# Column-tiled products issued in whole groups, state outputs four tiles side by side, and a buffer of its own for the S5 parameter scratch

## The chip, the cores and the metric

The kernel runs on one core of one Trainium2 chip. Its time is that of the device, in microseconds (us), from one execution of the whole program; several executions are timed and their median is compared. Engines are named as in the profile: PE is TensorE (PEld its weight loads), DVE is VectorE, ACT is ScalarE, POOL is GpSimd, SP is SyncE, which here only issues DMA transfers.

## The reference

One layer of a decoder works on 256 prompt tokens and 64 sample tokens (eight sequences of eight) with the same weights, model width 2048, all in float32. Cut to what the change touches:

```python
h = _rmsnorm(x, p['norm_mix'])
z = h @ p['w_in']                       # one projection of 11280 columns, split into:
u_s5, q_g, k_g, v_g, r_g, a_low, q_x, gate_logits = jnp.split(z, ...)
# S5: 64 groups of 16 channels, each with 64 complex states; h_re, h_im from a scan over time
bu_re = jnp.einsum('blgc,gpc->blgp', ug, bbar_re)      # and bu_im
y = (jnp.einsum('blgp,gcp->blgc', h_re, c_re)
     - jnp.einsum('blgp,gcp->blgc', h_im, c_im) + d_skip * ug)
# attention over 256 memory tokens, 4 heads of 256; the sample has its own cached keys and values
scores = jnp.einsum('blhd,bmhd->bhlm', qh, mem_k) * (XA_HEAD_DIM ** -0.5)
o = jnp.einsum('bhlm,bmhd->blhd', jax.nn.softmax(scores, axis=-1), mem_v)
# then gated linear attention, the merge of the three branches, w_out, and a SwiGLU of 5632
```

The memory keys and values of the prompt are themselves a product of the normalised memory with `w_mem_k` and `w_mem_v`, and are outputs too.

## The kernel before

Activations lie with features on the 128 partitions and the 320 tokens as columns. A block of weights of 128 x 2048 (a unit) is loaded by SP into one of three `raw` buffers, and `parts` (L73 to L81) makes two numbers of each: `whi` (a cast on ACT, L79) and `wlo` (the rest, a subtraction on DVE, L80), two buffers of each. `mm3` (L87 to L93) multiplies them with activations that are split in the same way: three matmuls per 128 rows (L91, L92, L93), 48 for a unit of 16 blocks. `proj` is one unit of `w_in` with the activations `hh` and `hl`.

The program has three parts. `front` (L205) makes the memory's values (8 steps, L298 to L300) and keys (8 steps, `kT`, L342), and during the keys writes the normalised input: it scales a block (L348, DVE), casts it to `hh` (ACT) and subtracts to `hl` (DVE, both in `split`, L1066 and L1067). Beside it POOL works out the parameters of the S5 branch (`s5_params`, L365): some 140 small operations, then the doublings of the rotation table (L508 to L511) and the input map `bb` (L498 to L500). These use a scratch tile, `s5_scr`, that before the change has the tag `hl`: it lies in the very buffer in which `hl` is written afterwards (L243, L334). So the first `hl` has to wait until POOL has read `s5_scr` for the last time.

`body` (L1024) advances three generators, each with its share of steps: `main` (the attention over the memory, `attn`, for four heads, then the gated linear attention, `gla`), `s5` (eight tiles of 128 channels, `s5_tile`) and `gates` (48 projections). A scheduler with a model of times then puts the instructions of each engine in order. PE works off its order strictly: an instruction that waits holds all behind it. `back` (L1069) is merge, output projection and feed forward, nothing but units with `mm3`.

Some products are column-tiled: the stationary operand has only 32 columns, the product uses one of four 32-column strips of the array (`tile_position=(0, 32 * c)`), and four products that stand next to each other on four strips can run at the same time. They are in float32, and each one is two MATMUL rows in the trace. There are four kinds:

- `yp` (L654): outputs of the S5 states, 4 tiles of states times real and imaginary part, 8 products of 320 columns for each of 8 tiles of channels. Before, a tile goes through in two halves (`JB = 2`): after each half two tiles of states are multiplied, so no more than two strips are ever in use, in the order part 0 of both, part 1 of both.
- the sample's keys (L749) and values (L770) in `attn`: 16 products of 256 columns each, for each of 4 heads: two sets `g` of four sequences `c`, accumulated over two blocks. Keys and values come by DMA in pieces of two sequences into `at_kv`, three buffers (L739).
- the decay input (L809) and the sample's states in `gla` (L962), which the change leaves as they are.

Each is an instruction of its own to the scheduler, which may put others between them.

Of the kernel before, what the change touches and what calls it, by code (L numbers as in the profile page):

```python
# [49 lines left out]
class Build:  # L50
# [32 lines left out]
    def unit(self, src, n=2048):  # L83
        """A block of weights in two parts that sum to it exactly."""
        return self.parts(self.load(src, n), n)
# [8 lines left out]

    def psum_mm(self):
        # the banks of the small products serve too once those are over
        self.turn += 1
        if self.wide and self.turn % 2:
            return self.psum_sm()
        return self.pmm.tile([P, 512], F32, name="pmm", tag="pmm", bufs=2)  # L100
# [11 lines left out]
    def rstd_tok(self, out, sums, n, scale):  # L112
        """out[token, tile] = 1 / sqrt(scale sum over partitions of sums + eps); sums may be several."""
# [16 lines left out]
        # a step of third order, then one of Newton's  # L130
# [10 lines left out]
    def spread(self, r, n):  # L141
        """PSUM [128, n]: r[token, tile] in the columns of its tokens, on all partitions."""
# [9 lines left out]
    def rstd(self, sums, n, scale):  # L152
        """The same by columns, in PSUM; sums has whole tiles of columns."""
# [4 lines left out]
    def build(self):  # L158
        nc, tc, io = self.nc, self.tc, self.io
        with ExitStack() as es:  # L160
# [18 lines left out]
            # the activation table is loaded before the first operands come  # L179
            early = cp.tile([P, 1], F32, name="early")  # L180
            nc.scalar.activation(early[:], self.ones[:, 0:1], AF.Copy, scale=1.0)
            # the tensor engine's clock rises with use, ahead of the first operands
# [7 lines left out]
            # scan resets of a chunk of the prompt and of the sample  # L190
# [14 lines left out]
    def front(self):  # L205
# [37 lines left out]
        params = self.s5_params(mp, hp.tile([P, KD * NT], F32, name="s5_scr", tag="hl", bufs=1))  # L243
# [8 lines left out]
        def load(i):  # L252
            """Weights of a step; with the first four, the memory of the same rows."""
# [28 lines left out]
        def products(i):  # L282
# [5 lines left out]
            # values: tokens on partitions  # L288
# [22 lines left out]
        with self.tc.manual_schedule(engines={mybir.EngineType.SP}):  # L311
            load(0)
            load(1)
            for i in range(16):
# [15 lines left out]
                if i == 6:  # L330
# [3 lines left out]
                    self.hl = hp.tile([P, KD, NT], F32R, name="hl", tag="hl", bufs=1)  # L334
# [6 lines left out]
                # keys: features on partitions  # L341
# [23 lines left out]
    def s5_params(self, tp, scr):  # L365
        """Decay, rotations and input map of the states, 64 of a group on 64 partitions."""
# [44 lines left out]
        # sine and cosine: reduced by multiples of pi/2, then polynomials  # L411
# [40 lines left out]
        # sin = sg (s ev + c odd), cos = sg (c ev - s odd)  # L452
# [15 lines left out]
        # reciprocal, from its bits and by Newton steps  # L468
# [16 lines left out]
        # rotations, first 16 steps of all states  # L485
        for n in (1, 2, 4, 8):
            self.double(self.tab1, 32, n, *(scr[:, o : o + 64 * n] for o in (2048, 2048 + 512)), V)

        # input and output maps, two groups of channels side by side
# [12 lines left out]
    def double(self, tab, nj, n, x, y, V):  # L502
        """Steps n+1..2n of the rotations in tab from steps 1..n."""
# [9 lines left out]
    def s5_prep(self, ut):  # L513
        """Input of one tile of 128 channels and the map of its four tiles of states."""
# [6 lines left out]
        # products of 32 channels: rows hi, lo, hi of u by rows hi, hi, lo of the map  # L521
# [29 lines left out]
    def s5_tile(self, ut, prep):  # L551
        """Generator over the steps of one tile of 128 channels, four tiles of states."""
# [14 lines left out]
        # |a| e^(i theta CH): carries a state from a chunk to the next  # L567
# [6 lines left out]
        # initial states of the sample, turned to the positions in its chunk  # L574
# [14 lines left out]
        yp = self.pmm.tile([P, 512], F32, name="yp", tag="yp", bufs=1)  # L589
        for r0 in range(0, 4, JB):  # L590
# [42 lines left out]
            hp = []  # L633
            for i in range(JB):
# [7 lines left out]
                h = sp.tile([P, 2, NT], F32, name="s5_h", tag="s5_h", bufs=2)  # L642
# [8 lines left out]
            for part in range(2):  # L651
                for i in range(JB):
                    r = r0 + i
                    nc.tensor.matmul(  # L654
                        yp[32 * r : 32 * r + 32, :NT], self.cT[:, part, r, :], hp[i][:, part, :],
                        start=part == 0, stop=part == 1, tile_position=(0, 32 * r),
                    )
            if r0 + JB < 4:
                yield
        y = self.y1[:, ut, :]  # L660
# [19 lines left out]
    def attn(self, h):  # L680
# [9 lines left out]
        def softmax(ps, n, rows):  # L690
            """Rows of ps[:rows, n, 256] to probabilities in SBUF."""
# [16 lines left out]
        # prompt  # L708
# [27 lines left out]
        # sample: keys as [b, d-tile, mem], values as [b, mem-tile, d]; four sequences side by side,  # L736
        # each in 32 rows of which the first 8 count
        def cache(b, which):
            kv = ap.tile([P, 2, 512], F32, name="at_kv", tag="at_kv", bufs=3)  # L739
# [4 lines left out]
        for g in range(2):  # L744
            kv = [cache(4 * g, 0), cache(4 * g + 2, 0)]
            for i in range(2):
                for c in range(4):
                    b = 4 * g + c
                    nc.tensor.matmul(  # L749
                        ps[32 * c : 32 * c + 32, g * 256 : (g + 1) * 256],  # L750
                        q[:, i, NP_ + b * SL : NP_ + b * SL + 32], kv[c // 2][:, c % 2, i * 256 : (i + 1) * 256],
                        start=i == 0, stop=i == 1, tile_position=(0, 32 * c),
                    )
# [577 lines left out]
```

## Time and profile before

| | us |
|---|---|
| median of three runs | 2143.52 (2142.88 to 2143.59) |
| span of the profiled execution, first to last instruction | 2141.8 |
| PE busy | 2113.7 (99%) |
| DVE busy | 1293.9 (60%) |
| ACT busy | 849.1 (40%) |
| POOL busy | 147.1 (7%) |

For the profiled execution only its span is given; the runs' median is 1.7 us longer, which lies ahead of the first and behind the last instruction. Busy time is the union of an engine's instructions. A matmul's listed duration runs to its modelled end and overlaps with the next one's; what PE spends on one is read from the distance of two starts.

### The profile page before, as it was taken

To read this page: it belongs to the slowest core of one execution; us is meant where nothing else is said; L and a number is where in the kernel's file an instruction comes from. 1 tells how busy PE (TensorE), PEld (TensorE's weight loads), DVE (VectorE), ACT (ScalarE), POOL (GpSimd) and SP (SyncE) were. 2 spreads that over 40 slices of the span, in tenths; PEclk is the share of its full clock that TensorE was granted. 3 is DMA by queue.
4 is the path that set the end of the run, shared out by engine and by line. 5 is a ranking of instruction groups with operands and counts; after the bars stand their busy time and mean duration, and the time that the engine had idled before them with its cause. 6 is when DMAs were issued, how large, how long until landed. Compare 5 with 4: busy or idle time off the path is not lost.

```text
span 2141.8 us, 34011 instructions
## 1 busy us (share of the span) xinstructions
PE 2113.7 (99%) x14404; PEld 2047.6 (96%) x14404; DVE 1293.9 (60%) x1964; ACT 849.1 (40%) x1117; POOL 147.1 (7%) x203
## 2 busy tenths in 40 slices
PE   9899999999999999999999999999999999999997
PEld 7799898989999999999999999999999999999997
DVE  7768769898897864675555444444444444444444
ACT  6444344564444333554433333233322333233343
POOL 8511011011011000000000000000000000000000
PEclk9899999999999999999999999999999999999998
DMA  9565654436345454675554444454435443444442
GB/s 331 198 218 196 212 212 166 155 130 198 128 156 172 134 187 151 219 242 194 188 206 143 150 141 146 136 172 154 141 128 167 158 153 124 149 170 153 145 135 104
DMA packets 72697, 362.23 MB, mean 169 GB/s; under 512 B 8032, under 2 KB 18144, under 8 KB 42720
## 3 DMA queue, kind: packets, MB, share of 16 engines
q1 hardware_dynamic: 72544, 360.05, 49.3%
q8 instruction: 113, 1.85, 0.4%
q14 instruction: 40, 0.33, 0.0%
HBM read 338.49 MB, written 21.53 MB: 168 GB/s over the span
## 4 chain that ended last, share of the span: by engine, by line
PE 94%; POOL 3%; DVE 1%; ACT 1%; issue 1%; DMA 0%; DVEq 0%; POOLq 0%
PE pmm L93 20%; PE pmm L91 20%; PE pmm L92 19%; PE psm L91 10%; PE psm L93 10%; PE psm L92 10%; PE yp L654 1%; PE bu L600 0%; PE psm L770 0%; PE psm L749 0%; PE psm L896 0%; POOL s_ep L384 0%; PE psm L712 0%; PE psm L730 0%; DVE wlo L80 0%
## 5 line engine op out<-in xcount | busy, mean ns | idle before, releaser
L79 ACT CAST whi<-raw 128x2048 fp32r<-128x2048 f32 (+3 forms) x308 | 538.8, 1750 | 945.8 <-issue 542.8
L80 DVE TENSOR_TENSOR wlo<-raw,whi 128x2048 fp32r<-128x2048 f32 (+3 forms) x308 | 649.6, 2110 | 293.1 <-ACT whi L79 287.4
L93 PE MATMUL pmm<-hh,wlo 128*128 128x320 f32 x1408 | 439.8, 312 | 0.0
L91 PE MATMUL pmm<-hh,whi 128*128 128x320 f32 x1408 | 439.5, 312 | 0.0
L92 PE MATMUL pmm<-hl,whi 128*128 128x320 f32 x1408 | 438.1, 311 | 0.0
L93 PEld LDWEIGHTS pmm<-hh,wlo 128*128 128x128 f32 x1408 | 264.5, 188 | 10.1 <-issue 9.2
L91 PEld LDWEIGHTS pmm<-hh,whi 128*128 128x128 f32 x1408 | 264.6, 188 | 7.5 <-issue 6.6
L92 PEld LDWEIGHTS pmm<-hl,whi 128*128 128x128 f32 x1408 | 264.5, 188 | 5.2 <-issue 4.8
L91 PE MATMUL psm<-fh,whi 128*128 128x320 f32 x704 | 217.6, 309 | 0.0
L91 PE MATMUL pmm<-fh,whi 128*128 128x320 f32 x704 | 217.6, 309 | 0.0
L92 PE MATMUL pmm<-fl,whi 128*128 128x320 f32 x704 | 217.6, 309 | 0.0
L93 PE MATMUL psm<-fh,wlo 128*128 128x320 f32 x704 | 217.5, 309 | 0.0
L92 PE MATMUL psm<-fl,whi 128*128 128x320 f32 x704 | 217.5, 309 | 0.0
L93 PE MATMUL pmm<-fh,wlo 128*128 128x320 f32 x704 | 217.5, 309 | 0.0
L91 PEld LDWEIGHTS psm<-fh,whi 128*128 128x128 f32 x704 | 132.1, 188 | 0.1
L92 PEld LDWEIGHTS pmm<-fl,whi 128*128 128x128 f32 x704 | 132.1, 188 | 0.0
L91 PEld LDWEIGHTS pmm<-fh,whi 128*128 128x128 f32 x704 | 132.1, 188 | 0.0
L93 PEld LDWEIGHTS pmm<-fh,wlo 128*128 128x128 f32 x704 | 132.1, 188 | 0.0
L92 PEld LDWEIGHTS psm<-fl,whi 128*128 128x128 f32 x704 | 132.1, 188 | 0.0
L93 PEld LDWEIGHTS psm<-fh,wlo 128*128 128x128 f32 x704 | 132.1, 188 | 0.0
L93 PE MATMUL pmm<-hidh,wlo 128*128 128x320 f32 x352 | 109.2, 310 | 0.0
L91 PE MATMUL psm<-hidh,whi 128*128 128x320 f32 x352 | 108.8, 309 | 0.0
(431 smaller groups left out, 3707.8 us busy)
## 6 DMA issues: line engine op xcount, KB each, us to landing
raw<-w_in SPq DMA_DIRECT2D x88, 1024.0 KB, 5.0
raw<-w_fg SPq DMA_DIRECT2D x44, 1024.0 KB, 4.9
raw<-w_fu SPq DMA_DIRECT2D x44, 1024.0 KB, 4.9
raw<-w_fd SPq DMA_DIRECT2D x64, 704.0 KB, 4.1
raw<-w_br SPq DMA_DIRECT2D x24, 1024.0 KB, 4.9
at_kv<-kv SPq DMA_DIRECT2D x32, 512.0 KB, 4.3
raw<-w_out SPq DMA_DIRECT2D x16, 1024.0 KB, 4.9
raw<-w_mk SPq DMA_DIRECT2D x8, 1024.0 KB, 5.3
```

The lines of the kernel that those rows point to most:

```text
L79: nc.scalar.copy(hi[:, s], raw[:, s])
L80: nc.vector.tensor_tensor(lo[:, s], raw[:, s], hi[:, s].bitcast(F32), op=ALU.subtract)
L91: nc.tensor.matmul(ps, hi[:, ws], xh[:, kx + k, :], start=k == 0, stop=False)
L92: nc.tensor.matmul(ps, hi[:, ws], xl[:, kx + k, :], start=False, stop=False)
L93: nc.tensor.matmul(ps, lo[:, ws], xh[:, kx + k, :], start=False, stop=k == nk - 1)
L654: nc.tensor.matmul(yp[32 * r : 32 * r + 32, :NT], self.cT[:, part, r, :], hp[i][:, part, :], start=part == 0, stop=part == 1, tile_positio ...
```

## The change

Three edits. First, a helper `together` gives its first product to the scheduler and asks that the others be issued right after it. The keys' products of a head are given as one group of 16, and so are the values'; the group starts with the product that needs the piece loaded last (`g = 1`, `c = 3`). All four pieces of keys (or values) are loaded first, and `at_kv` has four buffers instead of three. Second, the outputs of the states are no longer multiplied after each half: the four `s5_h` of a tile are kept (four buffers instead of two), and eight products follow as one group, imaginary part first, four strips side by side. Third, `s5_scr` gets a tile of its own, 2048 wide, in the pool of `front`; the doublings use its columns 1024 to 2047, the same that the input map uses for its two products, so the map's first product now stands behind the doublings on POOL. The scratch that the program keeps for DMA descriptors is set to 1024. Comments and docstrings are gone, which shifts line numbers by 7 or 8.

```diff
+    def together(self, products):
+        first = products[0]().ins
+        with self.tc.issue_after(first):
+            for p in products[1:]:
+                p()
...
-        params = self.s5_params(mp, hp.tile([P, KD * NT], F32, name="s5_scr", tag="hl", bufs=1))
+        params = self.s5_params(mp, mp.tile([P, 2048], F32, name="s5_scr"))
...
-                    self.hl = hp.tile([P, KD, NT], F32R, name="hl", tag="hl", bufs=1)
+                    self.hl = hp.tile([P, KD, NT], F32R, name="hl")
...
         for n in (1, 2, 4, 8):
-            self.double(self.tab1, 32, n, *(scr[:, o : o + 64 * n] for o in (2048, 2048 + 512)), V)
+            self.double(self.tab1, 32, n, *(scr[:, o : o + 64 * n] for o in (1024, 1536)), V)
...
-        yp = self.pmm.tile([P, 512], F32, name="yp", tag="yp", bufs=1)
+        hp = []
         for r0 in range(0, 4, JB):
...
-            hp = []
             for i in range(JB):
...
-                h = sp.tile([P, 2, NT], F32, name="s5_h", tag="s5_h", bufs=2)
+                h = sp.tile([P, 2, NT], F32, name="s5_h", tag="s5_h", bufs=4)
...
-            for part in range(2):
-                for i in range(JB):
-                    r = r0 + i
-                    nc.tensor.matmul(
-                        yp[32 * r : 32 * r + 32, :NT], self.cT[:, part, r, :], hp[i][:, part, :],
-                        start=part == 0, stop=part == 1, tile_position=(0, 32 * r),
-                    )
             if r0 + JB < 4:
                 yield
+        yp = self.pmm.tile([P, 512], F32, name="yp", tag="yp", bufs=1)
+        self.together([
+            lambda part=part, r=r: nc.tensor.matmul(
+                yp[32 * r : 32 * r + 32, :NT], self.cT[:, part, r, :], hp[r][:, part, :],
+                start=part == 1, stop=part == 0, tile_position=(0, 32 * r),
+            )
+            for part in (1, 0) for r in (3, 0, 1, 2)
+        ])
...
-            kv = ap.tile([P, 2, 512], F32, name="at_kv", tag="at_kv", bufs=3)
+            kv = ap.tile([P, 2, 512], F32, name="at_kv", tag="at_kv", bufs=4)
...
-        for g in range(2):
-            kv = [cache(4 * g, 0), cache(4 * g + 2, 0)]
-            for i in range(2):
-                for c in range(4):
-                    b = 4 * g + c
-                    nc.tensor.matmul(
-                        ps[32 * c : 32 * c + 32, g * 256 : (g + 1) * 256],
-                        q[:, i, NP_ + b * SL : NP_ + b * SL + 32], kv[c // 2][:, c % 2, i * 256 : (i + 1) * 256],
-                        start=i == 0, stop=i == 1, tile_position=(0, 32 * c),
-                    )
+        kv = [cache(b, 0) for b in range(0, SB, 2)]
+        self.together([
+            lambda g=g, i=i, c=c, b=4 * g + c: nc.tensor.matmul(
+                ps[32 * c : 32 * c + 32, g * 256 : (g + 1) * 256],
+                q[:, i, NP_ + b * SL : NP_ + b * SL + 32], kv[b // 2][:, b % 2, i * 256 : (i + 1) * 256],
+                start=i == 0, stop=i == 1, tile_position=(0, 32 * c),
+            )
+            for g in (1, 0) for i in range(2) for c in (3, 0, 1, 2)
+        ])
...
+        kv = [cache(b, 1) for b in range(0, SB, 2)]
+        self.together([
...
-    nc = _bacc.Bacc("TRN2", target_bir_lowering=False, num_devices=1)
+    nc = _bacc.Bacc("TRN2", target_bir_lowering=False, num_devices=1, dynamic_dma_scratch_size=1024)
```

The order of the instructions changes in all of the body. On PE, in the first head's attention, the first ten of the 16 keys' products stood together right behind the prompt's own products (L730); the other six came some 30 rows later, behind a product of the states:

```order
L93 MATMUL pmm<-hh,wlo 128x320
L91 MATMUL pmm<-hh,whi 128x320
L92 MATMUL pmm<-hl,whi 128x320
L654 MATMUL yp<-s_h,s_cT 32x320
L749 MATMUL psm<-at_kv,at_q 32x256 x6
L93 MATMUL pmm<-hh,wlo 128x320
```

Now all 16 stand where the ten stood (L738 is the prompt's product, L754 the keys'):

```order
L92 MATMUL pmm<-hl,whi 128x320
L738 MATMUL psm<-at_pT,v 128x256 x4
L754 MATMUL psm<-at_kv,at_q 32x256 x16
L93 MATMUL pmm<-hh,wlo 128x320
L91 MATMUL pmm<-hh,whi 128x320
```

The group is one piece in all four heads, for keys and for values. On PE at the end of the body, the last half tile of states before the change stood in three pieces (one product, then these two and one):

```order
L91 MATMUL pmm<-hh,whi 128x320
L92 MATMUL pmm<-hl,whi 128x320
L654 MATMUL yp<-s_h,s_cT 32x320 x2
L93 MATMUL pmm<-hh,wlo 128x320
L654 MATMUL yp<-s_h,s_cT 32x320
L91 MATMUL pmm<-hh,whi 128x320
```

Now the whole last tile is one piece:

```order
L91 MATMUL pmm<-hh,whi 128x320
L92 MATMUL pmm<-hl,whi 128x320
L662 MATMUL yp<-s_h,s_cT 32x320 x8
L93 MATMUL pmm<-hh,wlo 128x320
L91 MATMUL pmm<-hh,whi 128x320
```

So it is in six of the eight tiles; the first stands as 6, 1 and 1 with transposes between, the sixth as 4 and 4. Over the whole program PE goes over to column-tiled products from others 52 times before the change and 29 times after it. On SP, at the beginning of the body, the loads of the first head's keys and values (L740) stood as 3, 2, 2 among those of projection weights (L70) and stores of gates (L1021):

```order
L740 DMA at_kv<-kv 128x1024 x3
L70 DMA raw<-w_in 128x2048 x3
L1021 DMA d_gate<-gst 128x320
L70 DMA raw<-w_in 128x2048 x2
L1021 DMA d_gate<-gst 128x320
L70 DMA raw<-w_in 128x2048
L740 DMA at_kv<-kv 128x1024 x2
L1021 DMA d_gate<-gst 128x320
L740 DMA at_kv<-kv 128x1024 x2
L70 DMA raw<-w_in 128x2048 x2
```

Now they stand in fours (L748; L1028 is the store):

```order
L748 DMA at_kv<-kv 128x1024 x4
L70 DMA raw<-w_in 128x2048 x3
L1028 DMA d_gate<-gst 128x320
L70 DMA raw<-w_in 128x2048 x2
L1028 DMA d_gate<-gst 128x320
L70 DMA raw<-w_in 128x2048
L748 DMA at_kv<-kv 128x1024 x4
L1028 DMA d_gate<-gst 128x320
L70 DMA raw<-w_in 128x2048 x2
L748 DMA at_kv<-kv 128x1024 x4
```

The loads of a whole group stand ahead of two weights that had one of its halves before them. In `front` the order on PE, DVE, ACT and SP is the same as before; on POOL only the map's first product has moved behind the doublings.

## Rows read from the trace of the kernel before

**Rows 1.** Page: span, PE's busy time (share, instructions).

```profile
span 2141.8 us, 34011 instructions
PE 2113.7 (99%) x14404; PEld 2047.6 (96%) x14404; DVE 1293.9 (60%) x1964; ACT 849.1 (40%) x1117; POOL 147.1 (7%) x203
```

**Rows 2.** Busy time by stretch: stretch length, PE, PEld, DVE, ACT, POOL, PEclk, DMA, GB/s.

```profile
80.00:85.00 5.00, 0.77 (x2) 0.50 (x2) 3.61 (x5) 0.00 (x0) 1.28 (x2) 0.50 0.00 0
400.00:440.00 40.00, 40.00 (x267) 37.35 (x266) 38.65 (x73) 19.55 (x43) 0.00 (x0) 1.00 0.45 155
440.00:460.00 20.00, 18.74 (x130) 17.54 (x128) 18.71 (x48) 15.62 (x25) 7.54 (x5) 1.00 0.35 114
1210.00:2100.00 890.00, 890.00 (x6065) 889.18 (x6064) 401.24 (x386) 284.86 (x252) 0.00 (x0) 1.00 0.44 148
```

**Rows 3.** Chain that ended last, in order of time: start, us on it, what.

```profile
161.65 1.42 PE psm L749 x20
...
230.56 0.99 PE psm L749 x12
...
301.87 1.20 PE yp L654 x8
...
368.66 4.31 PE pmm L809 x59
...
409.03 0.66 PE yp L654 x2
414.28 1.19 PE yp L654 x6
...
474.98 0.57 PE psm L962 x8
```

**Rows 4.** PE's instructions around a piece of L654: start, duration, instruction.

```profile
172.74 0.31 PE L91 MATMUL pmm<-hh,whi 128*128 128x320 f32 x1
172.98 1.26 PE L654 MATMUL yp<-s_h,s_cT 128*32 128x320 f32 x6
174.18 0.42 PE L92 MATMUL pmm<-hl,whi 128*128 128x320 f32 x1
174.43 0.31 PE L93 MATMUL pmm<-hh,wlo 128*128 128x320 f32 x1
```

**Rows 5.** DVE in front: start, duration of all, instruction, [idle before <- releaser].

```profile
64.12 5.06 DVE L80 TENSOR_TENSOR wlo<-raw,whi 128x2048 fp32r<-128x2048 f32 x1 [0.98 <-ACT whi L79]
69.11 7.63 DVE L348 SCALAR_TENSOR_TENSOR xr<-xr,vec,rx 128x320 f32<-128x320 f32 x8
81.39 0.89 DVE L1067 TENSOR_TENSOR hl<-xr,hh 128x320 fp32r<-128x320 f32 x2 [4.65 <-POOL s_bb L500]
...
82.93 2.29 DVE L80 TENSOR_TENSOR wlo<-raw,whi 128x2048 fp32r<-128x2048 f32 x1
...
89.68 1.93 DVE L348 SCALAR_TENSOR_TENSOR xr<-xr,vec,rx 128x320 f32<-128x320 f32 x4
```

**Rows 6.** PE in front, the same columns.

```profile
82.76 0.55 PE L91 MATMUL pmm<-mh,whi 128*128 128x256 f32 x1 [8.03 <-DVE kT L342]
...
85.27 0.58 PE L93 MATMUL pmm<-mh,wlo 128*128 128x256 f32 x1 [1.74 <-DVE wlo L80]
```

**Rows 7.** Busy time by stretch, columns as in rows 2.

```profile
88.00:90.00 2.00, 2.00 (x11) 2.00 (x11) 2.00 (x2) 0.00 (x0) 0.00 (x0) 0.50 0.72 303
...
92.00:93.00 1.00, 1.00 (x11) 1.00 (x11) 0.00 (x0) 0.00 (x0) 0.00 (x0) 1.00 0.98 418
```

**Rows 8.** All waits of PE from 100 to 900 us: who for whom, us, times, longest.

```profile
PE bu L600 <- ACT s_wb L548: 1.3, 1, 1.3
PE psm L910 <- DVE gl_att L905: 0.7, 1, 0.7
```

**Rows 9.** Waits of all engines from 115 to 905 us, the same columns.

```profile
ACT whi L79 <- PE pmm L92: 139.5, 54, 6.4
```

**Rows 10.** Tile `at_kv`: time of its loads from issue to landing.

```profile
DMA to landing us min/median/max: 3.5/4.3/8.2
```

More of the change, by code (lines that the diff above doesn't have):

```diff
@@ L765, in attn @@
         po = self.psum_sm()
-        for g in range(2):
-            kv = [cache(4 * g, 1), cache(4 * g + 2, 1)]
-            for m in range(2):
-                for c in range(4):
-                    nc.tensor.matmul(
-                        po[32 * c : 32 * c + 32, g * 256 : (g + 1) * 256],
-                        prT[:, m, g * P + 32 * c : g * P + 32 * c + 32], kv[c // 2][:, c % 2, m * 256 : (m + 1) * 256],
-                        start=m == 0, stop=m == 1, tile_position=(0, 32 * c),
-                    )
+        kv = [cache(b, 1) for b in range(0, SB, 2)]
+        self.together([
+            lambda g=g, m=m, c=c, b=4 * g + c: nc.tensor.matmul(
+                po[32 * c : 32 * c + 32, g * 256 : (g + 1) * 256],
+                prT[:, m, g * P + 32 * c : g * P + 32 * c + 32], kv[b // 2][:, b % 2, m * 256 : (m + 1) * 256],
+                start=m == 0, stop=m == 1, tile_position=(0, 32 * c),
+            )
+            for g in (1, 0) for m in range(2) for c in (3, 0, 1, 2)
+        ])
         ot = ap.tile([P, 2, 256], F32, name="at_ot", tag="at_pT", bufs=1)
```

## The prediction

> **What bounds the kernel now.** I read the page first. PE is busy for 2113.7 of 2141.8 us [rows 1], so a change pays only where it takes work or standing time from PE; what it saves on DVE, POOL or a queue counts only if PE was waiting for it. The stretches show where PE stands. Behind the front it is busy without a gap: 890 of 890 us in the feed forward with 6065 matmuls, so 0.147 us for a matmul of 320 columns, and 40 of 40 in the middle of the body [rows 2]. In the whole body it waits for 2.0 us, in two places [rows 8]. The exception is around 80 us, where it is busy for 0.77 of 5 us and its clock is at half [rows 2]: 8.03 us wait for a `kT` of DVE and 1.74 us for a `wlo` [rows 6]. DVE itself stands there for 4.65 us, until POOL has read the scratch that shares a buffer with `hl` [rows 5]. The chain of waits then says what PE spends on the column-tiled products [rows 3].
>
> Two numbers from those views are needed below. A float32 product of 320 columns takes four passes, 4 x 320 / 2.4 GHz = 0.533 us, one of 256 columns 0.427 us, and a piece of them adds 0.13 us: a single one (x2, two rows each) takes 0.66 us and four on four strips (L962, x8, 256 columns) 0.57 us [rows 3]. So four strips cost what one costs; I call this a round. And a piece lengthens the matmul in front (0.24 instead of 0.147 us) and the one behind (0.25) [rows 4]: about 0.2 us for each time PE goes over and back.
>
> **State outputs.** Before, a half tile has four products on two strips. Taken whole (x8) it is two rounds of two, 1.20 us; split as x2 and x6 it is three rounds in two pieces, 0.66 + 1.19 = 1.85 us [rows 3]. Of the 16 half tiles in the chain four are whole, seven are split in this way, two fall apart in three pieces of a round each (1.98), one in two pieces with one round each (1.32), and two have their first product among the keys' products and share its time, which I count as 1.3 each (an estimate: the 1.19 of their second piece and a little). Sum: 4 x 1.20 + 7 x 1.85 + 2 x 1.98 + 1.32 + 2 x 1.3 = 25.6 us. After, a whole tile is eight products on four strips, two rounds in one piece: 1.20 us. Six of the tiles stand so; the one in 6, 1, 1 takes 1.20 + 0.66 + 0.66 = 2.52 us, the one in 4, 4 takes 1.32. Sum 11.0 us, a saving of 14.6. That four strips also run at the rate of one with 320 columns, and over many rounds, is in the row of L809: 32 products in eight rounds, 4.31 us [rows 3].
>
> The Trainium skill ("TensorE: Matmul & The Clock Gate", Measured speedup vs the span model) speaks against so full a gain: it gives 3.07 times for four packed products, not four. By that figure a round of four would take 4 x 0.533 / 3.07 = 0.69 us, and the saving would be some 3 us less; the row of L809 disagrees (0.54 us a round), and the trace decides.
>
> **Keys and values.** 16 products are four rounds. Before they came as ten and six: three rounds (1.42 us) and two (0.99), as 4 + 4 + 2 and 2 + 4 [rows 3]; 2.41 us, eight times (four heads, keys and values). In one piece of four rounds: 4 x 0.427 + 0.14 = 1.85 us. Saving 8 x 0.56 = 4.5 us.
>
> **Fewer pieces.** 52 changes to column-tiled products become 29; 23 x 0.2 us = 4.6 us. This is PE time in the body like the rest.
>
> **The scratch.** DVE no longer stands until 81.39 us but goes on at 76.74, where its eight scalings end [rows 5]. What follows in its queue until PE is supplied (two `hl`, `kT`, one `hl`, a `wlo`) took from 81.39 to 85.22, 3.8 us, with POOL idle. Now POOL is still at work, and under POOL's large operations DVE was half as fast: 7.63 / 8 = 0.95 us for a scaling against 1.93 / 4 = 0.48 without, 5.06 us for a `wlo` against 2.29 [rows 5]. At half speed the 3.8 us become 7.7, the `wlo` ends at 84.4 instead of 85.2, and PE gains 0.8 us. At full speed it would gain all of 4.65. In the worst case the two engines take turns for all that is left, 4.65 + 3.8 us from 76.74, which ends at 85.2: nothing gained. I take 1.0, next to the slowed rows. The clock: PE's grant was 0.50 at 88 to 90 us and 1.00 at 92 to 93 [rows 7], 11 matmuls in 2 us and in 1 us, so the stretch of some 6 us from 85.27 at half clock cost about 3 us. PE still stands for most of 75 to 84 us, so I expect the clock to fall again and count 0.5 us; 0 and 3 are the ends. Front together 1.5 us, from 0 to 7.6.
>
> The Trainium skill ("SBUF — State Buffer", Who interferes with whom) has the rule to the slowed rows: a DVE instruction with two inputs in SBUF contends with a POOL instruction that reads SBUF, and whoever is late blocks entirely. By it the gain is near the low end, since `hl` and `wlo` are of this kind; the trace agrees in size, 5.06 against 2.29 us.
>
> **What costs.** The memory reserve of the descriptors and the larger buffers add no instruction. The group waits for the last of its operands, and PE holds all behind it; before, the second piece waited for the same operand. For the states it is the fourth `s5_h`, as before. For the values of a head it is the last of four loads, which now all begin only when the keys' group has released the buffers. In the second head the order leaves the least room, by its rows at 0.147 us and the transposes some 9.7 us; four loads issued at 0.4 us and 8.2 us to the slowest landing [rows 10] need 9.8. So 0 to 2 us there, I take 0.5. And DVE: from 400 to 460 us it is busy for 57.4 of 60 us [rows 2]. About six half tiles fall into the stretches of 400 to 640 us in which DVE is as full as this; there I save about 8 us of PE's work (6 x 0.8 us and their pieces, with the neighbours), and where DVE can't follow, PE waits instead. I count a quarter, 2 us, from 0 to 8. What hides SP's new order is that weights are early: ACT's casts wait 139.5 us for PE to release buffers [rows 9], so loads that come some us later reach no one.
>
> **Sum.** 14.6 + 4.5 + 4.6 + 1.5 - 0.5 - 2.0 = 22.7 us off the profiled span of 2141.8: 2119.1. The median of the runs is 1.7 us above that span, so 2120.8, I say 2121.
>
> **Rivals.**
> - *DVE becomes the bound in the middle of the body.* For it: 97% busy from 400 to 440 us, and PE's only wait of the body over 1 us is next to it, where DVE had 94% [rows 2, 8]. Against: over the whole of the body DVE has room. Then all 8 us are lost and some of the other pieces with them: 2127 to 2133, say 2128.
> - *The front gives all it can.* POOL and DVE hardly meet, PE's gap shrinks to 3 to 4 us and its clock stays up: 7.6 instead of 1.5 us, and DVE follows in the body: 2121 - 6 - 2 = 2113. For it: POOL has only 4.65 us left. Against: the 5.06 us of the `wlo`.
> - *Slower: SP holds the weights back.* Four loads of a group wait as one block for the buffers of the group before, and two weights stand behind them that had half a group before them. If SP stands for so long that a weight's cast is no longer ahead of PE, PE waits at every group. To eat the gain of 23 us, each of the eight groups would have to cost 2.9 us on PE; ACT's longest wait for PE is 6.4 us [rows 9], so a delay of a weight by 6.4 + 2.9, about 9 us, at each group is the point from which it decides; at 12 us it is 8 x 5.6 = 45 us more and 2166. Against: no wait of PE for a load in the body [rows 8].
> - *The grouping does not hold on the chip*, four strips run like two: only the fewer pieces and the front remain, 4.6 + 1.5, plus half of the keys: 2135 to 2139. Against it are the rows of L809 and L962.
>
> **How the numbers follow.** My forecast, 2117 to 2125, has a chance of 0.50; the full front 0.20; DVE as the bound 0.18; four strips like two 0.05; the rest, no gain or slower by SP or by an order that happens to fit worse, 0.07. A range of 2112 to 2131 leaves out about 0.2. About 0.2% (4 us) is what a measurement tells from no change; faster by more than this 0.92, within it 0.04, slower 0.04.
>
> **What would show it.** In the profile after: `yp` as x16 pieces of 1.20 us and the keys and values as x32 pieces of 1.85 us; about 24 us less of PE between 95 and 890 us, and the same 890 us in the feed forward. In front, DVE going on at about 77 us without a wait for POOL, its `hl` near 0.9 us each and the `wlo` over 4 us, and PE's two waits of together 9.8 us shrunk by 1 to 2 us with the clock still at half about 88 us. I am wrong if a round of four takes over 0.6 us, if PE shows waits of over 5 us in the body, on DVE or on a load, or if front ends more than 4 us earlier or no earlier at all.

## The result and the profile after

The changed kernel takes 2118.03 us (median of 4 runs, 2116.72 to 2122.14), the kernel before, run beside it, 2143.41 us (2142.88 to 2143.59): a ratio of 0.9884, 95% interval 0.9872 to 0.9897. The forecast was 2121 us, 2112 to 2131. The profiled execution has a span of 2116.4 us against 2141.8 [rows 1], 25.4 us less.

The page of after, its lines on busy time and its chain of waits by engine:

```profile
span 2116.4 us, 34013 instructions
...
PE 2088.3 (99%) x14404; PEld 2039.8 (96%) x14404; DVE 1294.6 (61%) x1964; ACT 848.8 (40%) x1117; POOL 161.3 (8%) x203
...
PE 91%; DVE 6%; ACT 1%; issue 1%; DMA 1%; SPq 0%; DVEq 0%; ACTq 0%
```

PE has the same number of instructions and 25.4 us less busy time [rows 1]; it stands idle for 28.1 us in both, so the whole difference is time in which PE worked, of which part is the clock. The chain that ended last gives the pieces (start, us, what), to be set beside [rows 3]:

```profile
154.72 1.86 PE psm L754 x32
172.03 1.86 PE psm L775 x32
...
289.44 1.21 PE yp L662 x16
...
357.91 1.19 PE pmm L816 x10
```

The keys' product is now line 754, the values' 775, the state outputs' 662, the decay input's 816. Each of the eight groups of keys and values is one piece of 1.86 us (1.42 and 0.99 before); a whole tile of state outputs is one of 1.21. A new piece has come as well: the decay input, 32 products in a row before (x59 in that row, two rows a product), is now cut up by other work. The stretches that answer to [rows 2, 7]:

```profile
80.00:85.00 5.00, 4.44 (x39) 4.44 (x40) 5.00 (x5) 3.04 (x4) 4.84 (x4) 1.00 0.69 241
85.00:90.00 5.00, 1.53 (x12) 1.16 (x10) 5.00 (x4) 2.31 (x3) 3.14 (x3) 1.00 0.25 103
...
92.00:94.00 2.00, 2.00 (x11) 2.00 (x11) 2.00 (x6) 1.59 (x4) 0.00 (x0) 0.50 0.83 352
...
400.00:440.00 40.00, 40.00 (x289) 38.93 (x288) 31.42 (x73) 27.10 (x52) 9.11 (x5) 1.00 0.44 150
440.00:460.00 20.00, 20.00 (x139) 18.33 (x138) 17.69 (x41) 8.62 (x17) 0.00 (x0) 1.00 0.38 130
1185.00:2075.00 890.00, 890.00 (x6065) 889.18 (x6064) 401.11 (x385) 284.60 (x252) 0.00 (x0) 1.00 0.44 148
```

The feed forward is the same, 6065 matmuls in 890 us. From 400 to 460 us PE is busy without a gap, and DVE for 49.1 us instead of 57.4: it did not become the bound there (the same instructions lie some 12 to 16 us earlier now, and just ahead of this stretch DVE did hold PE up, as the waits below show). The hole in front has moved from 75 to 85 us to 85 to 90 us, and the half clock with it, to 92 to 94. DVE and PE in front (answering to [rows 5, 6]; start, duration of all, instruction, idle before):

```profile
61.24 2.45 DVE L80 TENSOR_TENSOR wlo<-raw,whi 128x2048 fp32r<-128x2048 f32 x1 [1.40 <-ACT whi L79]
63.62 4.96 DVE L355 SCALAR_TENSOR_TENSOR xr<-xr,vec,rx 128x320 f32<-128x320 f32 x8
68.50 1.36 DVE L1074 TENSOR_TENSOR hl<-xr,hh 128x320 fp32r<-128x320 f32 x2
...
72.98 4.77 DVE L1074 TENSOR_TENSOR hl<-xr,hh 128x320 fp32r<-128x320 f32 x5
...
80.43 5.40 DVE L355 SCALAR_TENSOR_TENSOR xr<-xr,vec,rx 128x320 f32<-128x320 f32 x4
...
87.02 3.35 DVE L80 TENSOR_TENSOR wlo<-raw,whi 128x2048 fp32r<-128x2048 f32 x1
```

```profile
80.56 0.38 PE L93 MATMUL pmm<-mh,wlo 128*128 128x256 f32 x1 [1.53 <-DVE wlo L80]
...
90.42 0.39 PE L93 MATMUL pmm<-mh,wlo 128*128 128x256 f32 x1 [3.64 <-DVE wlo L80]
```

DVE no longer waits for POOL; it goes on from the scalings to `hl` at 68.5 us. But from 70 us to 94 it is busy all the time, at 0.95 us for an `hl` and 1.35 for a scaling, and PE waits for its `wlo`: from 40 to 125 us it waits for 7.0 us in all, 6.8 of them in three waits for a `wlo`, where before it was 8.03 and 1.74. The waits of PE in the body (130 to 1080 us), where before there were two [rows 8]:

```profile
PE pmm L93 <- DVE wlo L80: 2.6, 1, 2.6
PE psm L969 <- DMA gl_s<-s: 1.6, 1, 1.6
PE bu L607 <- DVE s5Q L614: 0.8, 1, 0.8
PE bu L607 <- issue: 0.5, 1, 0.5
PE psm L729 <- DVE at_p L712: 0.4, 1, 0.4
```

The longest of them ends at 386 us. The weight's cast, its `wlo`, PE's row and the busy time of the eight microseconds before it (columns as in [rows 2]):

```profile
377.51 1.91 ACT L79 CAST whi<-raw 128x2048 fp32r<-128x2048 f32 x1
...
383.67 2.28 DVE L80 TENSOR_TENSOR wlo<-raw,whi 128x2048 fp32r<-128x2048 f32 x1
...
386.00 0.42 PE L93 MATMUL pmm<-hh,wlo 128*128 128x320 f32 x1 [2.56 <-DVE wlo L80]
...
378.00:386.00 8.00, 5.45 (x38) 5.19 (x36) 8.00 (x13) 5.50 (x6) 0.00 (x0) 1.00 0.27 109
```

The cast was done at 379.4 us; DVE, busy without a gap, came to this `wlo` 4.2 us later, and PE waited for it. ACT's casts wait for PE about as before [rows 9]:

```profile
ACT whi L79 <- PE pmm L92: 146.1, 55, 6.4
```

Where the 25.3 us went follows from adding up, over both traces, the time from each PE instruction's start to the next one's. **2.7 us** lie ahead of PE's 60th instruction (19.0 us before, 16.3 after), where the change has nothing yet; over all the profiles of this document it comes at 16.1 to 19.3 us, whichever the kernel, so this part is the execution's. **4.2 us** lie between the 60th and the 640th, the front (99.1 and 94.9 us). **18.3 us** lie in the body: state outputs 26.1 to 11.1, keys and values 18.7 to 14.9, matmuls next to a piece 8.6 us over the normal rate to 4.1 (83 of them, then 40), waits 2.1 to 5.95, and small terms against it (+1.3 in all: the cut decay input, the matmuls next to it, the other products).

### The profile page after: what moved, and what is told of

It reads as the page before. It is cut to its first block, busy times and chain, and to the rows that moved or that the text cites. A ratio compares the mean times of both kernels' runs of the same rounds, so it can differ in the third digit from the quotient of the medians.

```text
span 2116.4 us, 34013 instructions
## 1 busy us (share of the span) xinstructions
PE 2088.3 (99%) x14404; PEld 2039.8 (96%) x14404; DVE 1294.6 (61%) x1964; ACT 848.8 (40%) x1117; POOL 161.3 (8%) x203
## 4 chain that ended last, share of the span: by engine, by line
PE 91%; DVE 6%; ACT 1%; issue 1%; DMA 1%; SPq 0%; DVEq 0%; ACTq 0%
PE pmm L93 19%; PE pmm L91 19%; PE pmm L92 18%; PE psm L91 10%; PE psm L92 10%; PE psm L93 10%; DVE wlo L80 1%; DVE xr L355 0%; DVE s_w L626 0%; PE psm L903 0%; ACT whi L79 0%; PE psm L306 0%; PE psm L754 0%; PE bu L607 0%; PE psm L307 0%
## 5 line engine op out<-in xcount | busy, mean ns | idle before, releaser
L92 PE MATMUL pmm<-hidl,whi 128*128 128x320 f32 x352 | 108.8, 309 | 0.0
```

What stands on the lines that cost most here:

```text
L92: nc.tensor.matmul(ps, hi[:, ws], xl[:, kx + k, :], start=False, stop=False)
```

## The experiments

The kernel before was timed beside every run, at 2143.1 to 2143.8 us; so all ratios are to it, and medians of runs timed apart are compared only where they differ by several us.

**The scratch alone.** The kernel before with the buffer of its own and the smaller reserve. The doublings use the new columns, so on POOL the map's first product stands behind them; on the other engines the order is that of before.

```diff
-params = self.s5_params(mp, hp.tile([P, KD * NT], F32, name="s5_scr", tag="hl", bufs=1))
+params = self.s5_params(mp, mp.tile([P, 2048], F32, name="s5_scr"))
-self.hl = hp.tile([P, KD, NT], F32R, name="hl", tag="hl", bufs=1)
+self.hl = hp.tile([P, KD, NT], F32R, name="hl")
...
```

> The kernel before with the S5 scratch alone moved to a buffer of its own; products and their order stay as they were. Theory A (the trace of the changed kernel read on: DVE and POOL share the time of front better than half speed suggested, PE loses about 5 us there instead of 9.8): front ends 4 us earlier, 2139 (2138 to 2141), and DVE shows no wait for POOL before the first hl. Theory B (what was predicted: contention eats nearly all): 1 to 1.5 us, 2142. Theory C (the 2.7 us that the changed kernel had already won at 17 us, before POOL's scratch can matter, belong to the change): 6.9 us, 2136.5, and PE's clock at 12 to 16 us stays at full.

Measured: 2137.25 us, ratio 0.9973 (0.9965 to 0.9982), so 6.1 us. The profiled execution was its slowest (2140.99). Between PE's 60th and 640th instruction it takes 95.4 us against 99.1, so 3.7 us in the front, and its body is that of before (983.2 and 982.4 us). The time lies between A's and C's, and the interval (2135.9 to 2139.5 us) covers both. The sign that C names is missing in this execution: the granted clock is 0.82 at 12 to 14 us and 0.50 at 14 to 16, as before. The faster executions had a higher mean clock (0.997 at 2135.75 us, 0.995 in the profiled one, 0.993 or 0.994 in nearly all of the kernel before), so part of the 6.1 us is clock; where it was kept is not shown. DVE goes on to `hl` without a wait, 9.3 us earlier than before [rows 5]:

```profile
72.05 2.34 DVE L1067 TENSOR_TENSOR hl<-xr,hh 128x320 fp32r<-128x320 f32 x2
```

**All but the scratch.** The changed kernel with the two lines above and the columns of the doublings undone; the reserve stays.

> The changed kernel with the S5 scratch again in the buffer of hl; the grouped products stay. Theory A: 4 us slower than the changed kernel, 2122 (2121 to 2124), with PE's 8 us wait for kT back at about 75 us. Theory B: 2119. Theory C: 2125, with the clock at half at 12 to 16 us as in the kernel before.

Measured: 2127.11 us, 0.9925 (0.9912 to 0.9937): 9.1 us over the changed kernel, next to C's 2125 (5.5 over its second measurement below, where A has 4 and C has 7; the two are not told apart). PE's wait in front is back (the first row is PE's wait, the second DVE's for POOL):

```profile
PE pmm L91 <- DVE kT L349: 9.6, 1, 9.6
```

```profile
81.05 0.89 DVE L1074 TENSOR_TENSOR hl<-xr,hh 128x320 fp32r<-128x320 f32 x2 [10.18 <-POOL s_bb L507]
```

Of the 10.3 us between the two profiled spans (2126.7 and 2116.4), 4.5 are in the front (99.4 us for the same 580 instructions) and 1.2 ahead of it; of the 4.1 in the body 1.6 are 13 matmuls at half clock after a wait of 2.6 us at 391 us, which the changed kernel's execution does not have.

**The state outputs alone** (whole tiles on four strips, one piece; the rest as before, but for the smaller reserve).

```diff
-for part in range(2):
-    for i in range(JB):
...
+self.together([
...
+    for part in (1, 0) for r in (3, 0, 1, 2)
+])
```

> The kernel before with the state outputs alone issued as one group of eight on four strips; keys, values and the scratch stay. If the terms add up: 14.6 us less of PE for yp and 14 pieces fewer at 0.2 us, 17.4 us, less some 2 us of new waits: 2128 (2126 to 2130). If DVE in the middle of the body is the bound: 2132 or more, with PE waits of over 5 us on DVE between 400 and 640 us. If four strips don't pay beyond two: 2140.

Measured: 2127.37 us, 0.9923 (0.991 to 0.9937), 16.0 us, as the sum of the terms has it. In the profiled execution 14.6 us of this lie in the body. Its pieces of `yp` add up to 12.8 us instead of 26.1, its keys and values to 19.3 (18.7 before).

**Keys and values alone** (groups of 16 and four buffers for the loads, with the smaller reserve).

```diff
-kv = ap.tile([P, 2, 512], F32, name="at_kv", tag="at_kv", bufs=3)
+kv = ap.tile([P, 2, 512], F32, name="at_kv", tag="at_kv", bufs=4)
...
-for g in range(2):
-    kv = [cache(4 * g, 0), cache(4 * g + 2, 0)]
+kv = [cache(b, 0) for b in range(0, SB, 2)]
...
```

> The kernel before with keys and values alone as groups of 16 and four buffers for them; state outputs and the scratch stay. If the terms add up: 8 x 0.56 us of PE and 3 pieces fewer, 5.1 us: 2138.3 (2137 to 2140), each group 1.85 us. If the later loads of the values hold PE up: a wait of PE for a load of 0.5 to 3 us in each of four heads, 2140 to 2146.

Measured: 2142.82 us, 0.9994 (0.9985 to 1.0003): no change. The groups are what they should be, 7.46 us each for keys and values. The gain goes elsewhere (read in the profiled execution, the slowest, 2145.32 us): with the order that this part alone makes, the state outputs take 28.0 us instead of 26.1, and PE waits in the body for other things (the columns are who for whom, us, times, longest):

```profile
PE psm L968 <- DMA gl_s<-s: 2.6, 2, 2.1
PE psm L916 <- DVE gl_att L911: 0.7, 1, 0.7
PE pmm L93 <- DVE wlo L80: 0.7, 1, 0.7
```

The longest of these, at 873 us, is followed by half clock, 1.7 us more:

```profile
872.00:874.00 2.00, 0.73 (x9) 0.34 (x10) 1.54 (x1) 0.03 (x1) 0.00 (x0) 1.00 0.95 402
874.00:876.00 2.00, 2.00 (x10) 2.00 (x11) 0.00 (x0) 0.34 (x1) 0.00 (x0) 0.59 0.84 252
```

So not the loads of the values hid this gain, as the rival had it, but order and a load of another stage. The parts give 6.1, 16.0 and 0.5 us, 22.6 together; the whole gave 25.4, and 21.6 in its second measurement (the next paragraph). So the parts add up within that spread, and whether keys and values pay in the whole is not shown by a time: the changed kernel without them was not run.

**The whole groups without the hold.** `together` only calls the products.

```diff
-first = products[0]().ins
-with self.tc.issue_after(first):
-    for p in products[1:]:
-        p()
+for p in products:
+    p()
```

> The changed kernel, where `together` only calls its products in turn, without holding the others to the first. The order of TensorE's rows keeps all the whole groups (eight runs of 16 products for keys and values, the same pieces for the outputs), since the product that is ready last still comes first; only the 32 products of the decay input (L816) stand unsplit again, as before. Theory A: the gain is in the grouping, so it stays, and the split that goes gives back 5.37 - 4.96 = 0.4 us of changes of width and up to 1.3 us of waits for bu inside the split: 2116.5 to 2118. Rival B: the hold itself did something for the time (operands there when the group starts): slower than 2120.

What the expectation says of the decay input was wrong: the two programs have the same rows in the same order on every engine, the split of L816 and the waits too. So the hold does nothing here, and the groups come of the order in which the products and loads are given; that it is the product that is ready last, put first, is likely, but no run leaves that out alone. So this is a second measurement of the changed kernel, and it gives 2121.57 us (2118.44 to 2123.62), 0.9894 (0.9878 to 0.9909), 3.5 us over the first, with overlapping intervals. Between the two profiled executions (spans 2121.8 and 2116.4) the difference is nearly all the clock's. After the same wait for a `wlo` at 386 us the changed kernel (first fence) keeps its clock, and this one (second) does not:

```profile
385.00:387.00 2.00, 1.00 (x7) 1.00 (x8) 2.00 (x6) 0.82 (x2) 0.00 (x0) 1.00 0.16 16
...
389.00:391.00 2.00, 2.00 (x16) 2.00 (x15) 2.00 (x1) 0.00 (x0) 0.00 (x0) 1.00 0.54 225
```

```profile
385.00:387.00 2.00, 0.31 (x3) 0.05 (x1) 2.00 (x3) 1.84 (x2) 0.00 (x0) 1.00 0.04 8
...
389.00:391.00 2.00, 2.00 (x9) 2.00 (x9) 2.00 (x4) 0.00 (x0) 0.00 (x0) 0.50 0.68 266
```

It has three such stretches that the other lacks, at 13, 387 and 615 us, of 1.6, 1.7 and 1.9 us over the normal rate: 5.2 of the 5.4 us. The first follows a longer wait (1.70 us for a `whi` at 11 us, 0.31 in the other execution), the other two the same waits as there. What is left cancels: about 1 us for that longer wait, and a front of 93.9 us instead of 94.9.

**The reserve alone** (the kernel before with `dynamic_dma_scratch_size=1024`).

> The kernel before with nothing but the smaller scratch for dynamic DMA (1024). Theory A: it only frees memory; the first 17 us of the span, 2.7 us shorter in the changed kernel, came from the landing of the second piece of mraw, which varies: 2142.5 to 2144. Rival C: the smaller scratch is what lets that piece land earlier and keeps the clock up at 12 to 16 us: 2140 to 2141.

Measured: 2142.8 us, 0.9998 (0.9988 to 1.0007): no change, as A says. The order changes a little with the reserve (92 of PE's 14404 rows stand elsewhere). Its profiled execution also reaches the 60th instruction at 16.4 us with the full clock, though; what decides between some 16.3 and 19.1 us there is left to the execution, since the changed kernel has 16.3 and the same program's other execution, in the last paragraph, 19.1.

**Little on POOL.** The doublings and the map left out of the changed kernel (S5 is not computed), their tables filled.

```diff
-for n in (1, 2, 4, 8):
-    self.double(self.tab1, 32, n, ..., V)
+V.memset(self.tab1[:, :, :, 1:16], 0.5)
+V.memset(self.bb[:], 0.5)
...
```

> The changed kernel, but the doublings of the rotations and the input map of S5 on GpSimd (18 and 6 operations between 66 and 88 us) are left out and their two tables filled with a constant, so the S5 outputs are wrong. The order of TensorE's rows in the body stays. Theory A: what now bounds the front between 70 and 94 us is VectorE, and it is the bound because GpSimd works beside it: the subtractions hl go from 0.95 to 0.47 us, the scalings L355 from 1.35 to 0.50, the wlo from 2.5 and 3.35 to 2.3, some 9 us of VectorE in all, of which TensorE gets back its idle 7 us and perhaps 2 us of low clock behind it: 2109 to 2112. Rival B: VectorE is slow there for its own reasons (addresses, semaphores) or the chain over the releases of whi and wlo decides: 2116 or more, with hl near 0.95 still.

Measured: 2111.54 us, 0.9848 (0.9834 to 0.9863), and PE has no wait at all from 40 to 125 us. DVE's rows, to be set beside those of after:

```profile
65.97 3.79 DVE L355 SCALAR_TENSOR_TENSOR xr<-xr,vec,rx 128x320 f32<-128x320 f32 x8
...
73.41 2.10 DVE L1072 TENSOR_TENSOR hl<-xr,hh 128x320 fp32r<-128x320 f32 x5
...
77.95 1.94 DVE L355 SCALAR_TENSOR_TENSOR xr<-xr,vec,rx 128x320 f32<-128x320 f32 x4
...
86.94 2.29 DVE L80 TENSOR_TENSOR wlo<-raw,whi 128x2048 fp32r<-128x2048 f32 x1
```

0.42 us for an `hl` against 0.95, 0.48 for a scaling against 1.35, 2.29 for the last `wlo` against 3.35. The 580 instructions of the front take 85.0 us against 94.9. On every engine but POOL the order is that of the changed kernel. Theory A holds: POOL beside DVE costs the changed kernel's front 9.9 us (8.9 against its other execution).

**POOL's work later, and in two parts.** First all of it behind the fifth tile of keys, then only the last doubling and the map behind the sixth.

```diff
...
+V.tensor_scalar(scr[:, 1024:1025], self.kT[:, 4, 0:1], 1.0, None, op0=M)
 for n in (1, 2, 4, 8):
```

> The changed kernel, but GpSimd's doublings and map wait for the fifth tile of keys (kT[4], written at about 92 us, earlier if the front is faster), by a small operation that reads it; nothing is left out. Theory A: GpSimd then works beside VectorE where that has idle time (it is busy 4.9 of 10 us from 100 us on), VectorE runs alone between 66 and 88 us as in the run with little on GpSimd, the front ends 5 to 9 us earlier, and the map is done at about 105 us, ahead of its first reader at about 110: 2109 to 2113. Rival B: contention only moves (two or three wlo at 3.4 us) or the first bd is late for the map: 2115 to 2121. Rival D: VectorE bounds the front whatever GpSimd does: 2118.

> The changed kernel, but GpSimd's work between 66 and 88 us is cut in two: the first three doublings and the load of the map stay where they are, the last doubling and the map wait for the sixth tile of keys (kT[5]), by a small operation that reads it; nothing is left out. From TensorE's 60th to its 640th instruction the changed kernel took 94.9 us, the run with little on GpSimd 85.0, the one with all of GpSimd's work behind kT[4] 90.3, where VectorE was caught beside GpSimd at 84 to 95 us, one tile of keys too early. Theory A (VectorE is the bound while GpSimd works beside it): now the same 580 instructions take 86 to 89 us, and the median is 2112 to 2115. Rival B: the map ends too late for its first reader, TensorE waits 2 us or more for s_bd at the start of the body, and the 580 instructions take 90 us or more: 2116 to 2119.

Measured: 2117.05 us, 0.9878 (0.9861 to 0.9894), and 2113.99 us, 0.9863 (0.9848 to 0.9878). The front takes 90.3 and 88.0 us. The first was too early: POOL began at 84 us, where DVE had nothing to spare, and PE waited 2.7 us for a `wlo`; it is B that came. The second met A.

**More buffers in the body** (a third for `whi`, a second for `s0`).

```diff
-hi = self.wp.tile([P, 2048], F32R, name="whi", tag="whi", bufs=2)
+hi = self.wp.tile([P, 2048], F32R, name="whi", tag="whi", bufs=3)
...
```

> The changed kernel with a third buffer for whi and a second for the states s0 of the gated linear attention, in memory that the smaller scratch for dynamic DMA frees. Theory A: the body's waits that the change left (2.6 us for a wlo whose whi had no buffer, 1.6 us for gl_s, 0.8 us for s5Q: 5.95 us with the small ones) fall to 2 to 3 us, and with the long gaps go the stretches at half clock that followed them in other runs (1.6 to 1.9 us each): 2112 to 2116. Rival B: whi wasn't short of buffers; the wait is for VectorE's place in its order, and stays or moves: 2117 to 2120. Rival C: ACT's earlier whi puts more work beside GpSimd in the front, which then ends later than 111 us at the 640th instruction: over 2118.

Measured: 2113.98 us, 0.9862 (0.9846 to 0.9879). All that is left of PE's waits from 125 to 1070 us:

```profile
PE bu L607 <- ACT s_wb L555: 0.4, 1, 0.4
```

The body's instructions take 957.7 us against 964.1, 5.6 of it the waits. The time is in A's range, its cause is not shown: with the buffers the order changed on all engines (the first row of PE to differ is the 147th), and the two edits were not run apart. The wait at 386 us was not one for a free `whi`: that weight's cast was done 3.3 us before PE used it, and the `wlo` came late by its place behind other work of DVE (the rows of after). Of the 6.4 us, 2.9 are lost again behind the body: PE waits 2.1 us for a `wlo` until 1171 us, and 1.8 go in a stretch at half clock behind that, less some small gains.

**Both, at two times.** Last, POOL in two parts together with the buffers, held back by the sixth tile of keys or by the fifth.

> The changed kernel with both edits that each gave about 4 us: GpSimd's last doubling and map behind kT[5], and a third buffer for whi with a second for s0. Theory A: they act in different places (front, body), so they add: 2114.0 + 2114.0 - 2118.0 = 2110.0, range 2108 to 2112, with the body at about 958 us of 7,000 instructions' ledger as with the buffers alone. Rival B: with the third buffer for whi the front is bound by VectorE also without GpSimd (it waited 3.8 us for kT there), and the first edit brings 1 us or less: 2113 to 2115.

> The same, but GpSimd's second part waits for kT[4], one tile of keys (some 5 us) earlier. Theory A (beside GpSimd every operation of VectorE costs up to twice its time while VectorE has none to spare, which it has only from about 92 us on): VectorE is caught in the sixth step's wlo and hl, TensorE waits 1 to 2 us more than in e11_both there, and 1 us less for s_bd: 2110 to 2113, 0 to 2 us above e11_both. Rival B: the wait for s_bd is what matters, and the earlier start is faster by 1 us: 2108 to 2110.

Measured: 2109.64 us (2106.8 to 2111.61), 0.984 (0.9826 to 0.9853), as the sum of the two gains, and 2105.49 us (2103.8 to 2110.78), 0.9827 (0.9813 to 0.984). The median of the earlier start is 4.2 us lower, below both theories' ranges, but the intervals overlap; it is 12.5 below the changed kernel. Of the 4.1 us between the two profiled executions 1.9 lie ahead of PE's 60th instruction, where the edits have nothing yet, 2.1 in the front and none in the body; 3.3 are stretches at half clock that the later one has (at 13 and 78 us) and the earlier has not. Which of that is chance isn't settled by one profile each, and stays open. POOL's rows of the earlier one show why little was lost by it:

```profile
87.42 3.80 POOL L506 TENSOR_SCALAR s_scr<-kT 128x1 f32<-128x1 f32 x1 [12.36 <-DVE kT L349]
91.31 1.11 POOL L520 TENSOR_TENSOR s_scr<-s_tab 128x512 f32<-128x512 f32 x1
...
95.93 3.17 POOL L510 TENSOR_TENSOR s_scr<-s_scr,s_cr 128x512 f32<-128x512 f32 x1
99.07 1.06 POOL L511 TENSOR_TENSOR s_scr<-s_scr,s_ci 128x512 f32<-128x512 f32 x1
```

Here POOL came second: an operation on one column lasted 3.80 us (0.23 in the run with POOL in two parts and no more buffers) beside a `wlo` and four `hl` at their full speed, 2.28 and 0.42 us, and the third row lies beside another `wlo` (95.90 us, 2.28). POOL really began at 91 us, when DVE had little left of its full stretch; the `wlo` that started just behind its second row, at 91.39 us, took 3.17.

## Why the prediction was right, and where it was not

The sum came close partly by luck. Of the 22.7 us forecast, 21.2 were to come in the body and 1.5 in front; measured were 18.3 in the body, 4.2 in front, and 2.7 ahead of both that no term had and that are the execution's. A second measurement of the same program gave 2121.57 us, next to the forecast of 2121.

- **State outputs, -14.6 us:** -15.1. A round of four strips does cost what one costs; the whole tile is 1.21 us, and the rival that four strips run like two is out. The sum after is 11.1 us (11.0 forecast), that before 26.1 (25.6).
- **Keys and values, -4.5:** -3.8. The keys' groups of the first and the fourth head stood before in part among state outputs and took 2.33 and 1.96 us of their own instead of 2.41; the rest of their time is in the 26.1 above.
- **Fewer pieces, -4.6:** -4.5, 43 neighbours fewer at 0.1 us each.
- **Costs in the body, +2.5:** +3.8 of waits and +1.3 beside them that no term had, together twice the forecast. PE now waits 3.8 us for DVE, 1.6 for a load and 0.5 for neither (2.1 in all before). For DVE I priced 2.0 us, for the kind that came: the 2.6 us at 386 us are a wait for DVE in a stretch where it has no gap, and by PE's rows that place is 397.7 us in the kernel before, at the edge of the stretch from 400 us that I had named. Inside it PE waited for DVE no more. For the loads I priced the values'; they did get slower (6.3 us instead of 4.3 in the median [rows 10]) and reached no one, and it was a state's load that PE waited for, at 611 us. Taken together, the 5.4 us on DVE and the load are over the 5 us at which the prediction calls itself wrong, though no single wait is.
- **Front, -1.5 (0 to -7.6):** here the step failed, and by the prediction's own mark (more than 4 us earlier) it was wrong, if narrowly: 4.2 us, 5.2 in the program's other execution, 3.7 with the scratch alone. 2.7 of the 4.2 are waits of PE (9.8 to 7.0 us), most of the rest the clock. The step took 76.74 us, where DVE's scalings ended, as a fixed start, and priced DVE's work up to the next `wlo`, 3.8 us, at half speed, as the whole story. But the start was not fixed: with the old buffer DVE's wait ends when POOL ends, at 81.39 us if DVE comes to it at 76.74 and at 81.05 if it comes at 70.87 (the run of all but the scratch). In the changed kernel DVE started its `hl` 12.9 us earlier (68.5 instead of 81.4): 4.65 are the wait, 5.4 come of a `wlo` and scalings that took 7.3 us together instead of 12.6, with POOL held in its turn (2.51 us for its 128x128 at 61.5 us, 0.47 before), and 2.9 of this execution's earlier start. That put PE 14.8 us ahead at 78 us, the 2.7 of the start in it; and POOL's work ran on to 88.2 us instead of 81.4 and took it back over the next tiles of keys: 13.0 us ahead at 85, 6.9 from 95 on. The gain and the loss were both far larger than priced, and that what is left of them lies inside the range is luck. The slowing itself was right (0.95 us for an `hl` was forecast as near 0.9); the place was not, and no `wlo` took over 4 us.
- **The clock:** it fell again, as assumed, some 4 us later than the rows that were named (0.50 at 92 to 94 us), for 1.7 us of loss instead of some 3: 1.3 us less, where 0.5 was counted.
- **Rivals:** DVE as the bound of the whole middle of the body is out (PE 60 of 60 us from 400 on); for 2.6 us ahead of it DVE was the bound. SP did not hold the weights back: ACT's casts still wait for PE, 146.1 us, the longest 6.4 as before [rows 9]. The full front did not come, but the run with little on POOL shows that it was there, 9.9 us below.

The Trainium skill's rule ("SBUF — State Buffer", Who interferes with whom) that with two such operations whoever comes second blocks entirely agrees with the rows of both sides here: DVE at 0.95 instead of 0.42 us beside POOL, and POOL at 3.80 us for one column beside DVE. The Trainium skill's figure of 3.07 times for four packed products ("TensorE: Matmul & The Clock Gate", Measured speedup vs the span model) is one for packing by rows, with three products packed by columns within some 5 ns of that packing. It does not fit this kernel's pieces on column strips: by it a whole tile would take an estimated 1.5 us, and it took 1.21.

## What to carry to other kernels

Price a wait that goes by what the two engines still have to do side by side, to the end of the last one's work, not up to the next instruction: freeing DVE from POOL moved their meeting, and the meeting cost more than the wait had left to give. An instruction group on strips costs its rounds and two changes, so whole groups are worth making (26.1 to 11.1 us for the state outputs); here the order in which the products were given kept them whole, without a hold. A part that shows nothing in the total (keys and values: 0.5 us alone) can still have done what it should, 3.8 us less in its own pieces, and have lost it to the order that it makes, so look at the pieces in the trace before it is judged. And a wait that goes with one more buffer is not shown to be that buffer's: where the order changes too, read what the instruction stood behind.

## What the runs showed of the hardware that was not expected

- The same program, the same wait of PE at 386 us: in one execution the granted clock stays at 1.00 (2.4 GHz), in another it falls to 0.50 (1.2 GHz), at a cost of 1.7 us. Two such places, and one behind a wait that was longer in one of them, explain 5.2 of the 5.4 us between two executions of the same rows, so a difference of 2 us between two kernels here needs more than one profile. With all but 0.4 us of PE's waits gone from the body, the three runs with more buffers show no such stretch there.
- POOL's small operations are held as well: 128x512 elements took it 1.06 us, or 3.17 beside a `wlo` of 2.28 us that was not slowed. And they can be held by more than one operation: the 3.80 us for one column lasted through five of DVE's.
